# An encoder block on one core: an earlier fourth quarter, spread ends of the down-projection, a two-pass column block, and decay products shared between two engines

## The chip, the core and the metric

The kernel runs on one core of one Trainium2 chip. The core has a matrix engine (TensorE, PE in the profile), a vector engine (VectorE, DVE), a scalar engine (ScalarE, ACT), GpSimd (POOL), and queues that start DMA transfers (here SyncE, SP). Each engine works through its own list of instructions in order and waits at semaphores for the others. The metric is the device time of one execution in microseconds, the median over repeated runs.

## The reference

The block has three residual parts and a last normalisation, for 2048 positions and a width of 1024, all in float32:

```python
def block(x):
    x = x + mixer(x)            # short conv group + 4 gated-linear-attention heads, then w_out
    x = x + memory_cross_attention(x, mem)
    x = x + sq_relu_mlp(x)      # relu(rms_norm(x) @ w_up) ** 2 @ w_down
    return rms_norm(x, final_norm)

def gla_chunked(q, k, v, log_a):               # chunks of 64 positions, each head
    b = jnp.cumsum(la, axis=3)                 # running sum of the log decays in a chunk
    q_t = q * jnp.exp(b)                       # the two decay products that the change touches
    k_t = k * jnp.exp(-b)
    ...

def sq_relu_mlp(x, mlp_norm, w_up, w_down):
    h = rms_norm(x, mlp_norm) @ w_up           # 1024 -> 4096
    return jnp.square(jax.nn.relu(h)) @ w_down # 4096 -> 1024
```

The mixer's linear-attention part has four heads, forwards and backwards; the MLP has 4096 hidden units.

## The kernel before, in words

Activations are kept transposed, 128 channels on the partitions and positions along the free axis. Every float32 operand of a matrix product is cut in two by `split` (L117 and L118): ScalarE rounds it to a high part, VectorE subtracts that from it to get a low part, and `mm3` or `product` adds three matmuls, high by high, high by low and low by high. So behind every matmul there are a cast on ScalarE and a subtraction on VectorE, and those must come in time.

**Decays.** For each of the four heads a generator makes running sums of the log decays (`sums`: L397, the scans L400, copies L405 and L406, L407) and then, in `apply` (L422), multiplies their exponentials with k and q that come back from DRAM, 128x512 at a time, four products for each half of the positions, eight for a head. Its order is `sums(0)`, `apply(0)`, `sums(1)`, `apply(1)`. This runs beside the projections of the second half of the positions, whose results VectorE copies out of PSUM at L249. The matmuls of `mm3` stand at L145 to L147.

**MLP, up.** `token_side(hf)` and `weight_side(f)` make a scheme of seven products for a 2x2 block product (operands are sums and differences of quarters; for 16 values of f and two token halves hf). Four quarters of the tokens, a11, a12, a21, a22, are read from `x2d` and scaled (`quarter`, L956 and L960). Each quarter is kept in two 128x1024 tiles, either of the ST ring (two tiles of 8 KB a partition, `S2`) or of the RAW and CV rings (three each, `R2`). The weights of each f come into RAW and CV as well (L990). In a ring a tile is given out again when its last reader is done. a12 is needed by the second product in the list (`yield 2`); before, its load waits for the ST tile of a11.

**MLP, down.** The same scheme over four groups of hidden rows (`GROUPS`), 56 steps of four output tiles each (L1243); `half_steps` yields a step's operands, kept two steps ahead (`ahead`). Operand sums are made by GpSimd and VectorE (`combine`, through `add` at L928). The accumulators `acc` start as the residual, sixteen 128x1024 transfers from `x2d` (`load_acc`, L1218). `sums` holds partial sums u that belong to three of the four quarter outputs, so 24 additions `add(o, o, u)` follow the loop.

**Columns.** Four hidden tiles (`REST`) fit in no group. They are done behind the loop with plain `mm3`, in five column blocks of up to 512 positions: `column` adds 12 matmuls for each of eight output tiles d to `acc`, squares it, and sums the squares; `finish` makes the norm's factors and writes the block out. `between` runs the finish of the last block in between.

Where `tc.manual_schedule` is open (the five column blocks), PE and DVE keep the order in which the code is written; elsewhere, and for all other engines, a scheduler sets each engine's order from the program's dependencies and its own costs, so what a line issues can stand elsewhere on an engine than the code suggests.

Of the kernel before, what the change touches and what calls it, by code (L numbers as in the profile page):

```python
# [13 lines left out]
ALU = mybir.AluOpType  # L14
# [16 lines left out]
def block_kernel(ctx, tc, x, mem, wm, wv, wlg, wlog, wout, wxk, wxv, wxqT, wxo, wup, wdn,  # L31
# [342 lines left out]
    def gla_decay(h, res):  # L374
# [35 lines left out]
        def apply(hf):  # L410
# [4 lines left out]
            for T, z in ((K[hf], zk), (Q[hf], zq)):  # L415
                for bi in range(2):
# [5 lines left out]
                    nc.vector.tensor_tensor(out=T[:, sl], in0=T[:, sl], in1=r, op=ALU.mult)  # L422
# [541 lines left out]
    def token_side(hf):  # L964
# [5 lines left out]
        a21 = quarter(hf, 1, 0, S2())  # L970
        yield None
# [8 lines left out]
        a12 = quarter(hf, 0, 1, S2())  # L980
# [238 lines left out]

    halves = [slice(0, TB), slice(TB, 2 * TB)]  # L1220
# [3 lines left out]
    load_acc(range(4))  # L1224
    sums = [A4(F32, (P, 2, TB)) for _ in range(4)]
    for i in range(14 * len(GROUPS)):
# [3 lines left out]
        if i == 0:  # L1230
            load_acc(range(4, KT))
# [5 lines left out]
        for d in range(4):  # L1237
# [7 lines left out]
            o11, o21 = (acc[d][c][:, h] for h in halves)  # L1245
            o12, o22 = (acc[d + 4][c][:, h] for h in halves)
# [4 lines left out]
            for o in {1: (u,), 2: (o11,), 6: (u,), 5: (o22,), 3: (o12,), 7: (o21, o22), 4: (o21,)}[p]:  # L1251
                if p == 4:
                    add(o, o, ps, SUB)
                else:
                    add(o, ps, o)


    def rest_u(b):
        got = []
        for i in range(0, 4, 2):  # L1260
            t = (RAW() if i == 0 else CV()[:, :D]).rearrange("p (j t) -> p j t", j=2)
            for j in range(2):
                f = REST[i + j]
                nc.sync.dma_start(t[:, j], zu[f * P:(f + 1) * P, b * TB:(b + 1) * TB])
            hi, lo = (A4(F32R, (P, 2, TB)) for _ in range(2))
            split(t, hi, lo)
            got += [(hi[:, j], lo[:, j]) for j in range(2)]
        return got

    ur = [rest_u(0)]  # L1270
    wr = [load_w(wdn[f], T=G4) for f in REST]
    for d in range(4):
        for c in range(2):
            u = sums[d][:, c]
            for o in (acc[d][c][:, halves[1]], acc[d + 4][c][:, halves[0]], acc[d + 4][c][:, halves[1]]):
                add(o, o, u, eng=nc.vector)
# [13 lines left out]
    def column(us, c, cs, squares, between):  # L1290
# [3 lines left out]
        o = cs.start % TB  # L1294
        for d in range(KT):
            ds = slice(d * P, (d + 1) * P)
            ps = (PG if d % 2 == 0 else PS)()[:, :n]
            for j in range(4):
                mm3(ps, (wr[j][0][:, ds], wr[j][1][:, ds]), (us[j][0][:, o:o + n], us[j][1][:, o:o + n]), j == 0, j == 3)
# [94 lines left out]
```

## Time and profile before

| what | value |
|---|---|
| median of three runs | 2694.26 us (2693.18 to 2695.48) |
| profiled execution, its own time | 2702.45 us |
| its span | 2700.7 us |
| granted TensorE clock, mean | 0.983 |
| PE busy | 2592.5 us (96%) |
| VectorE busy | 1626.4 us (60%) |
| ScalarE busy | 933.2 us (35%) |
| GpSimd busy | 259.6 us (10%), 178 instructions |
| DMA | 353.26 MB, 131 GB/s in the mean |

Times in the profile are microseconds from the start of the span. A group's row gives the line, the engine, the operation, output<-inputs by the names of the tiles, partitions x elements, and the count, then busy time and mean nanoseconds of one. A timeline row begins with the start and the duration, and may end with the idle time ahead of it and what ended that, in brackets. A row of waits names who waited for whom, then the total in microseconds, the number of waits and the longest. PEclk is the clock that TensorE was granted, as a share of full speed. The stages lie at about 490 to 566 us (second half of the projections, with decays of heads 0 and 1), 1440 to 2038 (MLP up; its second token half from about 1727 on), 2034 to 2584 (MLP down), and 2584 to the end (column blocks).

### The profile page before, as it was taken

The page shows a single profiled execution, that of the slowest core. Times are in us where ns is not written, and L with a number is a line of the kernel's source. Part 1 is how long each engine was busy: PE and PEld are TensorE (multiplying, and loading weights), DVE is VectorE, ACT ScalarE, POOL GpSimd, SP SyncE. Part 2 cuts the span into 40 slices and gives each one's busy share as a digit, 9 for nine tenths or more (in the row PEclk, how much of TensorE's full clock was granted, in tenths as well). Part 3 has the DMA queues.
Part 4 walks back from the last instruction along what each step waited for, and adds up shares of the span by engine and source line. Part 5 has one row for each costly group of instructions (what it writes and reads, how often), then busy time and mean ns, then how long its engine had stood idle before and what let it go on. Part 6 is the DMA issues. An engine that isn't in the chain of part 4 may idle for free.

```text
span 2700.7 us, 34654 instructions
## 1 busy us (share of the span) xinstructions
PE 2592.5 (96%) x13560; PEld 2207.7 (82%) x13560; DVE 1626.4 (60%) x2502; ACT 933.2 (35%) x1432; POOL 259.6 (10%) x178
## 2 busy tenths in 40 slices
PE   7999999989989999999999999899999899999998
PEld 7898888877777787989997888788887788888877
DVE  6512363467766455344467657766556768687975
ACT  5411153434435343232234333433333223222232
POOL 0000000000010000000000000000003224243223
PEclk9999999999999999999999999999999999999999
DMA  7512354224435452111134333343338664555233
GB/s 253 179 61 69 101 185 162 81 88 121 135 104 175 145 183 94 52 43 48 48 115 166 106 113 106 110 159 107 112 121 290 220 197 150 179 168 174 95 106 110
DMA packets 198309, 353.26 MB, mean 131 GB/s; under 512 B 17345, under 2 KB 73793, under 8 KB 198145
## 3 DMA queue, kind: packets, MB, share of 16 engines
q1 hardware_dynamic: 198144, 351.05, 39.9%
q8 instruction: 106, 1.74, 0.3%
q14 instruction: 59, 0.48, 0.1%
HBM read 262.90 MB, written 88.08 MB: 130 GB/s over the span
## 4 chain that ended last, share of the span: by engine, by line
PE 77%; DVE 10%; DMA 6%; ACT 3%; issue 2%; POOL 0%; SPq 0%; DVEq 0%; POOLq 0%; ACTq 0%
PE ps L1013 12%; PE ps L145 9%; PE ps L147 9%; PE ps L146 9%; PE pg L1243 9%; PE ps L1243 9%; PE pg L1013 9%; PE pg L145 3%; PE pg L147 3%; PE pg L146 2%; DVE a L118 2%; DMA gt<-zv 2%; DVE g L118 1%; DVE st L474 1%; DVE g L400 1%
## 5 line engine op out<-in xcount | busy, mean ns | idle before, releaser
L145 PE MATMUL ps<-a,a 128*128 128x512 f32 (+1 forms) x840 | 306.0, 364 | 6.5 <-DVE t L249 5.9
L146 PE MATMUL ps<-a,a 128*128 128x512 f32 (+1 forms) x840 | 306.0, 364 | 0.0
L147 PE MATMUL ps<-a,a 128*128 128x512 f32 (+1 forms) x840 | 305.1, 363 | 0.0
L1243 PE MATMUL pg<-a,g 128*128 128x512 f32 x1176 | 288.6, 392 | 10.1 <-DVE a L928 7.2
L1013 PE MATMUL ps<-a,g 128*128 128x512 f32 x1152 | 284.5, 392 | 7.4 <-ACT a L117 4.4
L1243 PE MATMUL ps<-a,g 128*128 128x512 f32 x1176 | 284.8, 389 | 0.0
L1013 PE MATMUL pg<-a,g 128*128 128x512 f32 x1152 | 279.6, 390 | 1.7 <-ACT g L117 1.1
L1243 PEld LDWEIGHTS pg<-a,g 128*128 128x128 f32 x1176 | 221.7, 189 | 59.1 <-issue 7.6
L1013 PEld LDWEIGHTS ps<-a,g 128*128 128x128 f32 x1152 | 217.4, 189 | 54.1 <-ACT a L117 5.0
L1243 PEld LDWEIGHTS ps<-a,g 128*128 128x128 f32 x1176 | 220.8, 188 | 45.9
L1013 PEld LDWEIGHTS pg<-a,g 128*128 128x128 f32 x1152 | 216.4, 188 | 48.4 <-ACT g L117 2.0
L117 ACT CAST a<-raw 128x1024 fp32r<-128x1024 f32 (+1 forms) x126 | 127.9, 1022 | 346.0 <-PE ps L1243 112.1
L118 DVE TENSOR_TENSOR a<-raw,a 128x1024 fp32r<-128x1024 f32 (+1 forms) x126 | 156.0, 1246 | 117.3 <-ACT a L117 115.9
L117 ACT CAST g<-gt 128x512 fp32r<-128x512 f32 x180 | 103.8, 618 | 349.0 <-PE pg L1013 197.2
L145 PEld LDWEIGHTS ps<-a,a 128*128 128x128 f32 x840 | 161.6, 192 | 32.6 <-DVE t L249 4.7
L146 PEld LDWEIGHTS ps<-a,a 128*128 128x128 f32 x840 | 162.0, 193 | 23.2 <-issue 0.2
L147 PEld LDWEIGHTS ps<-a,a 128*128 128x128 f32 x840 | 161.7, 192 | 23.3 <-issue 0.2
L118 DVE TENSOR_TENSOR g<-gt,g 128x512 fp32r<-128x512 f32 x180 | 133.4, 780 | 44.7 <-ACT g L117 44.7
L928 POOL TENSOR_TENSOR gt<-gt,t 128x512 f32<-128x512 f32 x42 | 79.4, 1908 | 815.9 <-DMA t<-in_wdn 746.9
L928 DVE TENSOR_TENSOR t<-pg,t 128x512 f32<-128x512 f32 x64 | 44.2, 691 | 172.0 <-issue 126.3
L928 DVE TENSOR_TENSOR a<-pg,a 128x512 f32<-128x512 f32 (+1 forms) x128 | 84.1, 668 | 62.3 <-PE pg L1243 46.1
L118 DVE TENSOR_TENSOR g<-raw,g 128x1024 fp32r<-128x1024 f32 (+3 forms) x90 | 98.7, 1107 | 35.6 <-ACT g L117 35.5
(323 smaller groups left out, 5157.7 us busy)
## 6 DMA issues: line engine op xcount, KB each, us to landing
raw<-zu SPq DMA_DIRECT2D x64, 512.0 KB, 4.1
t<-in_wdn SPq DMA_DIRECT2D x84, 256.0 KB, 4.1
raw<-in_wm SPq DMA_DIRECT2D x32, 512.0 KB, 4.1
raw<-in_wup SPq DMA_DIRECT2D x32, 512.0 KB, 4.1
cv<-in_wup SPq DMA_DIRECT2D x32, 512.0 KB, 4.9
zu<-gt SPq DMA_DIRECT2D x64, 256.0 KB, 2.4
zu<-t SPq DMA_DIRECT2D x64, 256.0 KB, 3.9
cv<-zu SPq DMA_DIRECT2D x32, 512.0 KB, 5.0
```

What stands on the lines that cost most here:

```text
L117: mark["act"] = nc.scalar.copy(hi, src)
L118: nc.vector.tensor_tensor(out=lo, in0=src, in1=hi.bitcast(F32), op=ALU.subtract)
L145: nc.tensor.matmul(ps, lh, rh, start=first, stop=False)
L146: nc.tensor.matmul(ps, lh, rl, start=False, stop=False)
L147: mark["pe"] = nc.tensor.matmul(ps, ll, rh, start=False, stop=last)
L400: nc.vector.tensor_tensor_scan(out=Q[hf][:, sl], data0=reset, data1=K[hf][:, sl], initial=0.0, op0=ALU.mult, op1=ALU.add)
L474: nc.vector.scalar_tensor_tensor(out=St[r, a], in0=St[r, b], scalar=de[r, a:a + 1], in1=St[r, a], op0=ALU.mult, op1=ALU.add)
L928: eng.tensor_tensor(out=out, in0=a, in1=b, op=op)
L1013: nc.tensor.matmul(ps, W[w][:, ks], X[x][kt], start=first and kt + w + x == 0, stop=kt == 3 and w == 1, skip_group_check=not first)
L1243: nc.tensor.matmul(ps, l, r, start=not chained and k == 0 and l is wh and r is x[k][0], stop=k == n - 1 and l is wl, skip_group_check=chained)
```

## The change

Four things change.

First, a product of `apply` goes to GpSimd for heads 0 and 1 and stays on VectorE for heads 2 and 3: 16 of the 32 instructions move. Nothing else in the generator differs.

Second, in `token_side(1)` the quarter a12 is loaded right behind a21, into RAW and CV tiles; for the first half the code is as it was. On SyncE's queue, around the end of the first token half, this moves transfers. Before (raw and cv are the RAW and CV rings, st the ST ring, zu the hidden activations that go out, L990 the weights and L956 the quarters):

```order
L1019 DMA zu<-gt 128x512 x2
L1023 DMA zu<-t_13838 128x512
L990 DMA raw<-in_wup 128x1024
L1023 DMA zu<-t_13876 128x512
L990 DMA cv<-in_wup 128x1024
...
L1023 DMA zu<-t_14298 128x512
L990 DMA raw<-in_wup 128x1024
L990 DMA cv<-in_wup 128x1024
L956 DMA st<-x2d 128x2x512 x2
L1152 DMA st<-zu 128x2x512
```

And in the changed kernel, where L993 are the weights, from the same place on:

```order
L1022 DMA zu<-gt 128x512 x2
L1026 DMA zu<-t_13838 128x512
L956 DMA raw<-x2d 128x2x512
L1026 DMA zu<-t_13876 128x512
L956 DMA cv<-x2d 128x2x512
...
L1026 DMA zu<-t_13990 128x512
L993 DMA raw<-in_wup 128x1024
L1026 DMA zu<-t_14028 128x512
L993 DMA cv<-in_wup 128x1024
```

The two transfers of a12 stood, as st loads, behind four pairs of weight loads counted from the first of these rows; now they are a raw and a cv load in the place of the first of those pairs, and each pair of weights follows one place later.

Third, the beginning of the down-projection. The sixteen accumulator loads are issued at steps 0 and 2, eight each; before, eight were issued ahead of the loop and eight at step 0. Before, on SyncE's queue (a is an accumulator, t and gt tiles of the down weights, zu a hidden tile that is read back):

```order
L1171 DMA t_16721<-in_wdn 128x512
L1218 DMA a_16759<-x2d 128x1024
...
L1218 DMA a_16773<-x2d 128x1024
L1125 DMA cv<-zu 128x2x512
L1171 DMA gt<-in_wdn 128x512 x4
L1171 DMA t_16903<-in_wdn 128x512
```

In the changed kernel, from the first hidden tiles that the sums need:

```order
L1128 DMA raw<-zu 128x2x512
L1128 DMA cv<-zu 128x2x512
L1221 DMA a_16744<-x2d 128x1024
...
L1174 DMA t_16706<-in_wdn 128x512
L1221 DMA a_16750<-x2d 128x1024
...
L1221 DMA a_16758<-x2d 128x1024
L1174 DMA gt<-in_wdn 128x512 x4
```

The raw and cv tiles of the first hidden-row sum stand ahead of every accumulator, and the second eight accumulators, which stood ahead of the first gt weights, now come behind them and behind seven more weight transfers.

Fourth, the end of the down-projection. Operands of the first column block (`rest_u(0)`) and the first REST weights are asked for two steps before the loop ends. The 24 additions of u are made inside the first three column blocks, one for each d. The first column block goes through its eight output tiles twice: first with two of the four REST tiles, in all eight PSUM banks, then with the other two. The dictionary `goes` and `out_` say the same as the lines that they replace. On VectorE, before (g is a low part of a REST weight, the a rows with two a inputs are the additions of u, those with pg or ps take a product out of PSUM):

```order
L118 TENSOR_TENSOR g_20862<-raw,g_20861 128x1024
L928 TENSOR_TENSOR a_16709<-ps,a_16709 128x512
L928 TENSOR_TENSOR a_16773<-ps,a_16773 128x512
L118 TENSOR_TENSOR g_20868<-raw,g_20867 128x1024
L928 TENSOR_TENSOR a_16697<-a_16697,a_16711 128x512
L928 TENSOR_TENSOR a_16761<-a_16761,a_16711 128x512
...
L928 TENSOR_TENSOR a_16773<-a_16773,a_16714 128x512
L118 TENSOR_TENSOR a_20901<-raw,a_20900 128x1024
L118 TENSOR_TENSOR a_20908<-cv,a_20907 128x1024
L928 TENSOR_TENSOR a_16695<-pg,a_16695 128x512
```

In the changed kernel:

```order
L118 TENSOR_TENSOR g_20863<-raw,g_20862 128x1024
L928 TENSOR_TENSOR a_16758<-ps,a_16758 128x512
L928 TENSOR_TENSOR a_16943<-ps,a_16943 128x512
L118 TENSOR_TENSOR g_20869<-raw,g_20868 128x1024
L118 TENSOR_TENSOR a_20878<-raw,a_20877 128x1024
L118 TENSOR_TENSOR a_20885<-cv,a_20884 128x1024
L928 TENSOR_TENSOR a_16746<-a_16746,a_16696 128x512
L928 TENSOR_TENSOR a_16744<-pg,a_16744 128x512
L928 TENSOR_TENSOR a_16750<-a_16750,a_16697 128x512
L928 TENSOR_TENSOR a_16748<-ps,a_16748 128x512
L928 TENSOR_TENSOR a_16754<-a_16754,a_16698 128x512
L928 TENSOR_TENSOR a_16752<-pg,a_16752 128x512
```

The row of fourteen additions between the second weight and the first product is gone from there; each of them stands ahead of one product of the column block, and the splits of two weights and of the next operands come directly behind one another.

The diff, with the body of `rest_u` left out (it is moved up unchanged):

```diff
@@ -419,7 +419,7 @@
                     for o in (0, 64):
                         nc.sync.dma_start(r[o:o + 64], z[pr][r0:r0 + 64, c0:c0 + TB])
                     sl = slice(bi * TB, (bi + 1) * TB)
-                    nc.vector.tensor_tensor(out=T[:, sl], in0=T[:, sl], in1=r, op=ALU.mult)
+                    (nc.gpsimd if h < 2 else nc.vector).tensor_tensor(out=T[:, sl], in0=T[:, sl], in1=r, op=ALU.mult)
 
         sums(0)
         yield
@@ -968,6 +968,8 @@
         a11 = quarter(hf, 0, 0, S2())
         a22 = quarter(hf, 1, 1, R2())
         a21 = quarter(hf, 1, 0, S2())
+        if hf == 1:
+            a12 = quarter(hf, 0, 1, R2())
         yield None
         yield 1, operand(a11)
         yield 4, operand(a22)
@@ -977,7 +979,8 @@
         both(s, s, a11, ALU.subtract)
         yield 6, operand(s)
         both(a21, a11, a21, ALU.subtract)
-        a12 = quarter(hf, 0, 1, S2())
+        if hf == 0:
+            a12 = quarter(hf, 0, 1, S2())
         yield 2, operand(a12)
         yield 7, operand(a21)
         both(a12, a12, s, ALU.subtract)
@@ -1217,18 +1220,32 @@
                 acc[d][c] = A4()
                 nc.sync.dma_start(acc[d][c], x2d[d * P:(d + 1) * P, c * 1024:(c + 1) * 1024])
 
+    def rest_u(b):
...
     halves = [slice(0, TB), slice(TB, 2 * TB)]
     steps = half_steps()
     ahead = [next(steps)]
     acc = [[None, None] for _ in range(KT)]
-    load_acc(range(4))
     sums = [A4(F32, (P, 2, TB)) for _ in range(4)]
     for i in range(14 * len(GROUPS)):
         while len(ahead) < 3:
             ahead.append(next(steps, None))
         first, p, c, w, x = ahead.pop(0)
-        if i == 0:
-            load_acc(range(4, KT))
+        if i in (0, 2):
+            load_acc(range(2 * i, 2 * i + 4))
+        if i == 14 * len(GROUPS) - 2:
+            ur = [rest_u(0)]
+            wr = [load_w(wdn[REST[0]], T=G4)]
         n = len(x)
 
         chained = p in (2, 3)
@@ -1242,38 +1259,20 @@
                 for l, r in ((wh, x[k][0]), (wh, x[k][1]), (wl, x[k][0])):
                     nc.tensor.matmul(ps, l, r, start=not chained and k == 0 and l is wh and r is x[k][0],
                                      stop=k == n - 1 and l is wl, skip_group_check=chained)
-            o11, o21 = (acc[d][c][:, h] for h in halves)
-            o12, o22 = (acc[d + 4][c][:, h] for h in halves)
+            out_ = lambda dd, h: acc[dd][c][:, halves[h]]
             u = sums[d][:, c]
             if p == 1 and first:
                 nc.scalar.copy(u, ps)
                 continue
-            for o in {1: (u,), 2: (o11,), 6: (u,), 5: (o22,), 3: (o12,), 7: (o21, o22), 4: (o21,)}[p]:
+            goes = {2: ((d, 0),), 5: ((d + 4, 1),), 3: ((d + 4, 0),), 7: ((d, 1), (d + 4, 1)), 4: ((d, 1),)}
+            for o in [u] if p in (1, 6) else [out_(*g) for g in goes[p]]:
                 if p == 4:
                     add(o, o, ps, SUB)
                 else:
                     add(o, ps, o)
 
 
...
-    ur = [rest_u(0)]
-    wr = [load_w(wdn[f], T=G4) for f in REST]
-    for d in range(4):
-        for c in range(2):
-            u = sums[d][:, c]
-            for o in (acc[d][c][:, halves[1]], acc[d + 4][c][:, halves[0]], acc[d + 4][c][:, halves[1]]):
-                add(o, o, u, eng=nc.vector)
+    wr += [load_w(wdn[f], T=G4) for f in REST[1:]]
 
     def final_sums(sq, n, PT):
         m = n // P
@@ -1287,17 +1286,35 @@
         nc.vector.scalar_tensor_tensor(out=a, in0=a, scalar=g_fin[:, d:d + 1], in1=r, op0=ALU.mult, op1=ALU.mult)
         nc.sync.dma_start(out[d * P:(d + 1) * P, c * 1024 + cs.start:c * 1024 + cs.stop], a)
 
-    def column(us, c, cs, squares, between):
+    def column(us, c, cs, squares, between, passes=1):
 
         qs = []
         n = cs.stop - cs.start
         o = cs.start % TB
+        pss = []
+
+        def part(d, js):
+            ds = slice(d * P, (d + 1) * P)
+            for j in js:
+                mm3(pss[d], (wr[j][0][:, ds], wr[j][1][:, ds]), (us[j][0][:, o:o + n], us[j][1][:, o:o + n]), j == 0, j == 3)
+
+        for d in range(KT if passes == 2 else 0):
+            pss.append((PG if d % 2 == 0 else PS)()[:, :n])
+            part(d, (0, 1))
         for d in range(KT):
-            ds = slice(d * P, (d + 1) * P)
-            ps = (PG if d % 2 == 0 else PS)()[:, :n]
-            for j in range(4):
-                mm3(ps, (wr[j][0][:, ds], wr[j][1][:, ds]), (us[j][0][:, o:o + n], us[j][1][:, o:o + n]), j == 0, j == 3)
+            if passes == 1:
+                pss.append((PG if d % 2 == 0 else PS)()[:, :n])
+            part(d, (2, 3) if passes == 2 else range(4))
+            ps = pss[d]
             a = acc[d][c][:, cs]
+
+            if (c, cs.start) != (1, TB) and n == TB:
+                if cs.start == TB or d >= 4:
+                    add(a, a, sums[d % 4][:, c])
+                elif d < 4:
+                    dd = d + 4 * c
+                    late = acc[dd][1][:, halves[1]]
+                    add(late, late, sums[d][:, 1])
             add(a, ps, a)
             qs.append(GT()[:, :n])
             nc.scalar.activation(qs[-1], a, AF.Square)
@@ -1325,7 +1342,8 @@
         for n, (c, cs) in enumerate(blocks):
             if n + 1 < 4:
                 ur.append(rest_u(n + 1))
-            sq = column(ur[min(n, 3)], c, cs, nc.vector if n == len(blocks) - 1 else nc.gpsimd, todo)
+            sq = column(ur[min(n, 3)], c, cs, nc.vector if n == len(blocks) - 1 else nc.gpsimd, todo,
+                        2 if n == 0 else 1)
             for _ in todo or ():
                 pass
             todo = finish(c, cs, sq)
```

More of the change, by code (lines that the diff above doesn't have):

```diff
@@ L1218, in load_acc @@
                 nc.sync.dma_start(acc[d][c], x2d[d * P:(d + 1) * P, c * 1024:(c + 1) * 1024])
+    def rest_u(b):
+        got = []
+        for i in range(0, 4, 2):
+            t = (RAW() if i == 0 else CV()[:, :D]).rearrange("p (j t) -> p j t", j=2)
+            for j in range(2):
+                f = REST[i + j]
+                nc.sync.dma_start(t[:, j], zu[f * P:(f + 1) * P, b * TB:(b + 1) * TB])
+            hi, lo = (A4(F32R, (P, 2, TB)) for _ in range(2))
+            split(t, hi, lo)
+            got += [(hi[:, j], lo[:, j]) for j in range(2)]
+        return got
     halves = [slice(0, TB), slice(TB, 2 * TB)]
@@ L1255, in block_kernel @@
                     add(o, ps, o)
[L1258 to L1268, printed above, removed]
-    ur = [rest_u(0)]
-    wr = [load_w(wdn[f], T=G4) for f in REST]
-    for d in range(4):
-        for c in range(2):
-            u = sums[d][:, c]
-            for o in (acc[d][c][:, halves[1]], acc[d + 4][c][:, halves[0]], acc[d + 4][c][:, halves[1]]):
-                add(o, o, u, eng=nc.vector)
+    wr += [load_w(wdn[f], T=G4) for f in REST[1:]]
     def final_sums(sq, n, PT):
```

## The prediction

> **What bounds the kernel now.** I read the page's head first.
>
> ```profile
> span 2700.7 us, 34654 instructions
> PE 2592.5 (96%) x13560; PEld 2207.7 (82%) x13560; DVE 1626.4 (60%) x2502; ACT 933.2 (35%) x1432; POOL 259.6 (10%) x178
> raw<-in_wup SPq DMA_DIRECT2D x32, 512.0 KB, 4.1
> ```
>
> TensorE is busy for 96%, so the time is the time of its matmuls plus its idle stretches. An edit on another engine can win only what TensorE idles, or loses to a lower clock, at the place of the edit. So the second view is a table of stretches. Its columns are the stretch, its length, the busy time and count of PE, PEld, DVE, ACT and POOL, the granted clock, the DMA share and GB/s.
>
> ```profile
> core 0: us, PE busy (x) PEld busy (x) DVE busy (x) ACT busy (x) POOL busy (x), PEclk, DMA share, GB/s
> 514.00:532.00 18.00, 18.00 (x162) 18.00 (x161) 13.20 (x22) 12.12 (x12) 0.00 (x0) 1.00 0.43 145
> 532.00:562.00 30.00, 23.54 (x182) 22.96 (x181) 23.92 (x52) 14.71 (x15) 0.00 (x0) 0.94 0.33 102
> 1738.00:1758.00 20.00, 14.71 (x52) 11.35 (x51) 13.35 (x16) 9.94 (x13) 0.00 (x0) 0.83 0.44 127
> 1800.00:1820.00 20.00, 20.00 (x89) 16.49 (x89) 11.29 (x18) 7.31 (x12) 0.00 (x0) 1.00 0.41 131
> 2050.00:2060.00 10.00, 10.00 (x46) 8.29 (x45) 2.32 (x4) 5.48 (x10) 0.00 (x0) 1.00 1.03 410
> 2094.00:2114.00 20.00, 12.81 (x49) 10.13 (x48) 19.14 (x23) 4.50 (x5) 0.00 (x0) 0.83 0.83 280
> 2584.00:2604.00 20.00, 15.41 (x51) 10.85 (x51) 20.00 (x29) 4.09 (x5) 0.00 (x0) 0.83 0.43 108
> ```
>
> Count matmuls, not busy time, since a slow matmul counts as busy. The undisturbed stretch at 1800 has 89 of 128x512 in 20 us, 0.2247 us each. The three stretches like it at the places of the change have 52, 49 and 51, so they lose 37, 40 and 38 matmuls: **8.3, 9.0 and 8.5 us**. In each the clock is 0.83, so part of each loss is the slow clock after a long stop, which goes with the stop. The decays' stretch has 182 matmuls where the rate of the row before it (162 of 128x256 in 18 us, 0.111 us each) gives 270: **9.8 us**. All four together, 35.6 us, are a ceiling for what these edits can win at these places. What ends the longest waits in the MLP's two halves, from the list of waits (who for whom, total us, number, longest):
>
> ```profile
> PE ps L1013 <- ACT a L117: 4.4, 1, 4.4
> PE pg L1243 <- DVE a L928: 7.2, 1, 7.2
> ```
>
> **Part A, the quarter a12.** Its timeline, three engines together:
>
> ```profile
> 1724.28 0.33 SPq L990 DMA_DIRECT2D raw<-in_wup  x1
> 1728.59 1.22 DVE L118 TENSOR_TENSOR g<-raw,g 128x1024 fp32r<-128x1024 f32 x1
> 1733.87 1.22 DVE L928 TENSOR_TENSOR st<-st 128x1024 f32<-128x1024 f32 x1
> 1735.12 0.89 SPq L956 DMA_DIRECT2D st<-x2d  x2
> 1737.44 2.88 PE L1013 MATMUL pg<-a,g 128*128 128x512 f32 x12
> 1742.18 2.74 DVE L960 SCALAR_TENSOR_TENSOR st<-st,vec,rows 128x512 f32<-128x512 f32 x4 [5.29 <-DMA st<-x2d]
> 1744.73 0.51 PE L1013 MATMUL ps<-a,g 128*128 128x512 f32 x1 [4.41 <-ACT a L117]
> ```
>
> The load goes out at 1735.12, as the last reader of a11's tile ends (1733.87 + 1.22); it lands, is scaled until 1744.92 and cast, and TensorE, which was free at 1740.32, starts at 1744.73, at half clock for a while. In the changed kernel a12's transfers stand where the weights of the second half's f = 0 stood, two rounds of f earlier, so the load and the four scalings (2.74 us, on VectorE) are over some 40 us before. The price is one place for the weights: those of f = 1 now go out where 1724.28 stands, and land 4.1 us later (page row above) at 1728.4; with a cast (1.04 us, the ACT row under part C) their split can start at 1729.4 instead of 1728.59, so VectorE's list runs about 1 us late, to some 1738. Two splits of 1.22 us make a12's operands by 1740.4, against TensorE's 1740.32. No stop is left that is long enough to cost the clock. I keep 1 us for the a21 and a12 - s splits behind it, which VectorE now has to deliver without a pause: gain **7** of 8.3 (3 if the weights come late at each of the next f, 8.3 at most). GpSimd has no work in this stage (0.00 in both rows), so nothing there contends.
>
> **Part B, the start of the down-projection.**
>
> ```profile
> 2045.59 6.50 SPq L1218 DMA_DIRECT2D a<-x2d  x8
> 2059.10 4.31 SPq L1171 DMA_DIRECT2D t<-in_wdn  x4
> 2061.41 0.69 DVE L928 TENSOR_TENSOR a<-pg,a 128x512 f32<-128x512 f32 x1 [8.58 <-PE pg L1243]
> 2066.51 6.50 POOL L928 TENSOR_TENSOR gt<-gt,t 128x512 f32<-128x512 f32 x4 [646.65 <-DMA t<-in_wdn]
> 2074.02 7.42 DVE L118 TENSOR_TENSOR g<-gt,g 128x512 fp32r<-128x512 f32 x3
> 2081.37 4.58 DVE L118 TENSOR_TENSOR a<-st,a 128x1024 fp32r<-128x1024 f32 x2
> 2087.07 3.48 DVE L928 TENSOR_TENSOR st<-st,raw 128x1024 f32<-128x1024 f32 x1
> 2090.47 3.43 DVE L928 TENSOR_TENSOR st<-st,cv 128x1024 f32<-128x1024 f32 x1
> 2102.80 4.95 PE L1243 MATMUL pg<-a,g 128*128 128x512 f32 x12 [7.19 <-DVE a L928]
> ```
>
> The stop of 7.19 us names an addition out of PSUM on VectorE, which is itself at the end of a queue. While GpSimd works (from 2066.51 on), VectorE's instructions with two inputs in SBUF are stretched: three weight splits take 7.42 us, and without GpSimd six of them took 3.8:
>
> ```profile
> L118 DVE TENSOR_TENSOR g<-gt,g 128x512 fp32r<-128x512 f32 x6 | 3.8, 684 | 0.0
> ```
>
> So these three lose 7.42 - 2.05 = 5.4 us, the two st splits 4.58 - 2.44 = 2.1 and the two st sums 6.91 - 2.44 = 4.5 (1.22 alone, in part A): 12.0 us in a row. Yet just before, VectorE had idled 8.58 us in one wait. GpSimd starts late because the down weights stand behind eight accumulators of 512 KB, while the transfers are full (DMA share 1.03, 410 GB/s). The change takes those eight, 4 MB or 10 us at 410 GB/s, from ahead of GpSimd's inputs. The same 12 us of stretching then falls mostly where VectorE idles. I take **8** of 9.0. The other end: GpSimd's first sums now come while the first weight splits run, around 2034, and those feed the first matmuls; two of them stretched to 2.47 (7.42/3) cost 3.6 us there, and if in turn nothing is won at 2102, this part loses 2. So -2 to 9.
>
> **Part C, the end.**
>
> ```profile
> 2591.16 1.04 ACT L117 CAST g<-raw 128x1024 fp32r<-128x1024 f32 x1
> 2592.33 1.22 DVE L118 TENSOR_TENSOR g<-raw,g 128x1024 fp32r<-128x1024 f32 x1
> 2593.46 8.51 DVE L928 TENSOR_TENSOR a<-a,a 128x512 f32<-128x512 f32 x14
> L928 POOL TENSOR_TENSOR gt<-gt 128x512 f32<-128x512 f32 x21 | 27.4, 1307 | 63.7 <-ACT gt L1303 63.4
> ```
>
> Two things hold TensorE in 2584 to 2604: the weight splits, the last of which ends at 2593.55, and 14 additions behind them that keep the first product out until 2601.97. The first pass over eight banks needs two weights alone and has 8 x 6 matmuls, 10.8 us at 0.2247, which reaches past the splits of the other two. What the change pays: ten of the 24 additions ran beside full matmuls before and now all 24 stand in the columns. In the second pass TensorE gives a product each 6 x 0.2247 = 1.35 us; VectorE needs 8.51/14 = 0.61 for the addition and about the same for the product, 1.2 us, which fits. But GpSimd sums the squares at 1.31 us each (last row), and as part B shows the two-input addition and GpSimd's instruction hold each other up, so 0.61 + 1.31 = 1.9 us for each d against 1.35. Over eight d, GpSimd's sum ends 8 x 0.57 = 4.6 us late; the next block has 12 matmuls, 2.7 us, for each d, so it catches up there, and TensorE meets the delay only where it needs the squares. I charge 2.5 us: gain **6** of 8.5 (2 if all 4.6 and as much again land on TensorE's path, 8.5 if none).
>
> **Part D, the decay products.**
>
> ```profile
> L422 DVE TENSOR_TENSOR g<-g,gt 128x512 f32<-128x512 f32 x16 | 10.0, 687 | 3.2 <-ACT g L411 3.2
> L400 DVE TENSOR_TENSOR_SCAN g<-cst,g 128x256 f32<-128x256 f32 x16 | 9.7, 672 | 0.1
> 527.40 2.50 DVE L422 TENSOR_TENSOR g<-g,gt 128x512 f32<-128x512 f32 x4 [0.88 <-ACT g L411]
> 529.81 1.22 DVE L397 TENSOR_TENSOR g<-g,g 128x1024 f32<-128x1024 f32 x1
> 534.36 0.42 DVE L249 COPY t<-ps 128x256 f32<-128x256 f32 x1
> 557.72 0.58 PE L145 MATMUL ps<-a,a 128*128 128x256 f32 x1 [4.53 <-DVE t L249]
> ```
>
> The 16 products leave VectorE, 10.0 us in all, 2.5 for each half of a head; on GpSimd they take 1.31 each. TensorE waits here for the copies at L249, which stand behind `sums` in VectorE's list, which stood behind the products. Alone, L397 and what follows would start at once, and the copy at 534.36 would come 2.5 + 0.88 us sooner. But now four products on GpSimd (5.2 us) run at the same time as L397, four scans and L407, which all have two inputs in SBUF. If each pair excludes one another as in part B, the chain of 4.6 us (529.81 to 534.36) becomes 4.6 + 5.2 = 9.8 from 526.5 on, and ends at 536.3, 1.9 later than now; twice, -3 or -4. If scans run freely, it ends 3 us earlier and the 4.53 us wait with its slow clock is mostly gone: +8. No row shows a scan beside GpSimd, but VectorE's 128x512 subtractions and 128x1024 sums above all stretched, so I take the value near the lock with some slack, **0**.
>
> The Trainium skill, in "SBUF — State Buffer", section "Who interferes with whom", says that a VectorE instruction with two SBUF inputs contends with a GpSimd instruction that reads SBUF, and that the later one waits for the whole of the earlier. The rows of part B agree for subtractions and sums; for a scan no run here shows it. By that rule D would be the 0 or the loss, and the sum 21; by a rule that excepted scans, 29.
>
> **Sum.** 7 + 8 + 6 + 0 = 21 us. The profiled execution took 2702.45 us (1.75 more than its span) and would take 2681.5; it stands 8.2 above the median of the runs, and I carry the difference: 2694.26 - 21 = **2673**.
>
> **Rivals.** *More comes free:* scans don't contend, and the column block adds no waits. For it: only subtractions and sums were seen to stretch. Against it: a scan reads two SBUF tiles like them. It adds 8 (D) and up to 4 (B and C whole): 2694.3 - 33 = 2661, 2657 to 2666.
> *The start of the down-projection gives nothing:* GpSimd's early sums stretch the first weight splits, at 2034, by as much as they spare at 2102; with half of A gone too, the gain is 3.5 + 0 + 6 = 9.5 and less where the column waits are at their bound: 2681 to 2689. For it: VectorE stands behind ScalarE's casts there anyway, and the DMA is full.
> *It doesn't do what it says:* a12 comes early, but the weights behind it late, so TensorE stops for w instead, and the other stops pass to the next item in VectorE's queue. Gain under 5: 2690 to 2694, within the 0.2% (5.4 us) that a measurement here can tell from no change.
> *Slower:* one mechanism, that VectorE and GpSimd exclude each other whole wherever the change put them side by side, in the decays and the columns. VectorE then loses 16 x 1.29 = 20.6 less the 10.0 it was spared, and 24 x 1.31 = 31 at the additions, 42 in all. It decides once more than 21 of these reach TensorE; all of it gives 2694 + 42 - 21 = 2715. Against it: VectorE idles 40% of the time, and in the later column blocks a d takes 2.7 us.
>
> **Chances.** The forecast 0.50 (its own range 2666 to 2682), more comes free 0.18, the start gives nothing 0.17, no effect 0.09, slower 0.06. The range of 2658 to 2690 holds the first three but for their edges; it leaves out the last two. Faster 0.85, same 0.09, slower 0.06.
>
> **What would show it.** A: 1738 to 1758 with 80 matmuls or more and clock 1.00, L960 of a12 before 1710. B: GpSimd's first sum before 2060, no PE wait over 2 us between 2090 and 2110. C: no clock under 1.00 in 2584 to 2604, additions of u one by one, and a wait of 1 to 4 us near the first `final_sums`. D: scans beside GpSimd of clearly over 672 ns; at 672 the first rival holds. Wrong is the forecast if PE's wait at any of A to C stays over 4 us, or if new stops of more than 5 us appear in the weights after a12 or in the second column block.

## The result

The changed kernel takes 2679.74 us in the median (2678.59 to 2681.76, 4 runs) against 2693.72 for the kernel before (2692.69 to 2695.48, 4 runs): ratio 0.9949, 95% interval 0.9933 to 0.9964. Timed again beside its variants it gave 0.9944 (0.9930 to 0.9957). So it is 14 to 15 us faster. The forecast was 21 us faster, 2673 in a range of 2658 to 2690: the direction and the range held, and the forecast gain was one and a half times the measured one.

Its page begins, in the same form as before:

```profile
span 2676.8 us, 34723 instructions
PE 2582.6 (96%) x13560; PEld 2202.0 (82%) x13560; DVE 1629.3 (61%) x2486; ACT 933.6 (35%) x1432; POOL 278.9 (10%) x194
```

Busy times hardly differ. GpSimd has 16 more instructions, VectorE fewer, and yet VectorE's busy time rose from 1626.4 to 1629.3 us. What differs is in the stretches (columns as before):

```profile
core 0: us, PE busy (x) PEld busy (x) DVE busy (x) ACT busy (x) POOL busy (x), PEclk, DMA share, GB/s
532.00:562.00 30.00, 23.29 (x173) 22.91 (x172) 22.51 (x40) 14.52 (x15) 14.77 (x12) 0.87 0.38 119
1738.00:1758.00 20.00, 20.00 (x90) 16.54 (x89) 19.37 (x26) 11.19 (x18) 0.00 (x0) 1.00 0.73 246
2024.00:2034.00 10.00, 8.11 (x26) 5.53 (x25) 5.25 (x8) 4.68 (x8) 1.70 (x1) 0.83 0.88 300
2070.00:2090.00 20.00, 20.00 (x90) 16.36 (x89) 19.89 (x19) 6.39 (x8) 9.39 (x4) 1.00 0.86 297
2094.00:2114.00 20.00, 20.00 (x90) 16.55 (x89) 14.28 (x17) 6.19 (x8) 8.98 (x7) 1.00 0.69 235
2584.00:2604.00 20.00, 18.43 (x88) 14.92 (x87) 17.18 (x23) 6.00 (x9) 11.88 (x9) 1.00 0.07 26
```

Three of the four stops are gone: 90, 90 and 88 matmuls at full clock where there were 52, 49 and 51. In the decays' stretch the change did the opposite: 173 matmuls instead of 182, and a mean clock of 0.87 instead of 0.94. And there is a new stop at about 2025: 26 matmuls in 10 us at a clock of 0.83, where the kernel before has 46 at full clock.

Both kernels have 13,560 matmuls, so the k-th matmul can be looked up in two traces and its start compared. The difference of the two starts changes only where one kernel loses or wins. This table gives that change in microseconds, stage by stage (stages by the clock of the first trace of before); each row is one profiled execution, set against the first profile of before. The rows below the first three are the experiments.

| profile | 10–512 | decays 512–586 | 586–1469 | A 1694–1841 | start of down 2000–2065 | B 2065–2195 | C 2570–2608 | columns after it, 2608–2693 |
|---|---|---|---|---|---|---|---|---|
| before, again | +0.2 | -0.2 | -2.8 | -0.5 | +0.9 | -0.8 | -0.4 | -0.1 |
| changed | +0.6 | +2.3 | -5.3 | -7.0 | +3.0 | -11.6 | -8.9 | +3.7 |
| changed, again | +0.7 | +2.2 | -1.5 | -6.9 | +0.1 | -11.3 | -7.9 | +5.2 |
| A alone | -0.9 | -0.4 | -4.9 | -7.8 | 0.0 | -0.6 | 0.0 | 0.0 |
| B alone | -1.3 | +1.1 | -7.5 | -0.4 | +0.4 | -11.3 | -1.7 | -0.5 |
| C alone | +0.5 | +2.2 | -5.3 | -0.4 | +1.0 | -0.9 | -8.9 | +5.2 |
| D alone | +0.7 | +2.1 | -6.0 | +0.1 | 0.0 | -0.2 | +0.3 | -0.5 |
| changed, D undone | -4.2 | 0.0 | -4.9 | -7.8 | +0.4 | -11.6 | -8.9 | +3.9 |
| D undone, no additions of u in the columns | -1.0 | +0.2 | -2.7 | -7.0 | +0.8 | -10.7 | -8.9 | -0.1 |
| only the second half's products on GpSimd | -1.3 | -2.4 | -7.8 | -7.0 | +0.8 | -10.4 | -8.9 | +5.2 |
| the same, 8 additions in the loop | -0.2 | -1.7 | -8.8 | -7.9 | +1.8 | -10.8 | -8.9 | +3.4 |
| the same, 16 additions in the loop | -1.3 | -4.3 | +1.4 | -7.0 | +0.6 | -10.9 | -8.9 | +2.0 |
| the last, GpSimd's share for all four heads | -1.9 | -1.2 | -3.5 | -7.8 | +1.3 | -10.7 | -8.9 | +0.6 |

The stages left out (1469–1694, 1841–2000, 2195–2570) never differ by more than 0.1. In 586–1469 (attention, projections, many short waits) even two profiles of one kernel differ by 2.8 and 3.8 us; nothing in the edits touches it. The first profile of before was long there, which is part of why it took 2702.45 us while the median run took 2694.

### The profile page after: what moved, and what is told of

Read it like the earlier page. It is cut to its first block, busy times and chain, and to the rows that moved or that the text cites. A ratio compares the mean times of both kernels' runs of the same rounds, so it can differ in the third digit from the quotient of the medians.

```text
span 2676.8 us, 34723 instructions
## 1 busy us (share of the span) xinstructions
PE 2582.6 (96%) x13560; PEld 2202.0 (82%) x13560; DVE 1629.3 (61%) x2486; ACT 933.6 (35%) x1432; POOL 278.9 (10%) x194
## 4 chain that ended last, share of the span: by engine, by line
PE 78%; DVE 10%; DMA 5%; ACT 3%; issue 3%; POOL 1%; SPq 0%; DVEq 0%; POOLq 0%; ACTq 0%
PE ps L1016 12%; PE pg L1260 10%; PE ps L1260 10%; PE ps L145 9%; PE ps L147 9%; PE ps L146 9%; PE pg L1016 9%; PE pg L145 3%; PE pg L147 3%; PE pg L146 3%; DVE a L118 2%; DMA gt<-zv 2%; DVE g L400 1%; DVE st L474 1%; DVE a L928 1%
## 5 line engine op out<-in xcount | busy, mean ns | idle before, releaser
L118 DVE TENSOR_TENSOR a<-raw,a 128x1024 fp32r<-128x1024 f32 (+1 forms) x128 | 161.8, 1270 | 125.3 <-ACT a L117 123.4
L153 POOL TENSOR_TENSOR sm<-sm,nhalf 128x2 f32<-128x2 f32 (+1 forms) x26 | 24.3, 933 | 991.0 <-DVE sm L151 991.0
L117 ACT CAST g<-raw 128x1024 fp32r<-128x1024 f32 (+3 forms) x90 | 85.4, 959 | 95.3 <-PE ps L146 17.4
```

Of the source, the lines that this page charges most:

```text
L117: mark["act"] = nc.scalar.copy(hi, src)
L118: nc.vector.tensor_tensor(out=lo, in0=src, in1=hi.bitcast(F32), op=ALU.subtract)
L153: nc.gpsimd.tensor_tensor(out=r, in0=v, in1=nhalf[:, :n], op=ALU.pow)
```

## The experiments

**The four parts, one at a time.** Each is the kernel before with one part.

A:

```diff
+        if hf == 1:
+            a12 = quarter(hf, 0, 1, R2())
...
-        a12 = quarter(hf, 0, 1, S2())
+        if hf == 0:
+            a12 = quarter(hf, 0, 1, S2())
```

> The kernel before with the earlier quarter a12 alone. Theory (the prediction's step A, and the two traces, whose distance shrinks by 7.0 us across this place): 7 us less than before, ratio 0.9974; 1738 to 1758 at clock 1.00 with some 89 matmuls; nothing changes at 2094 and 2584. Rival (the weights behind a12 come late instead): under 3 us, with new waits of TensorE for casts of weights between 1730 and 1800.

Measured 2687.68 against 2696.83 us, ratio 0.9965 (0.9953 to 0.9977); at its own place 7.8 us in the trace. The theory holds, the rival falls: no new wait for weights. (One wait of 0.53 us for the split of a12's operand is new.)

B:

```diff
-    load_acc(range(4))
...
-        if i == 0:
-            load_acc(range(4, KT))
+        if i in (0, 2):
+            load_acc(range(2 * i, 2 * i + 4))
```

> The kernel before with the accumulator loads at steps 0 and 2 alone (the changed lookup of the outputs comes with it, since an accumulator may not exist yet when it is named). Theory: the stop at 2095 to 2107 goes (about 9 us), and a new one of 2 to 3 us appears at the first down-projection matmul, because the first weights stand behind four hidden-tile loads: net 6 to 9, ratio 0.997 to 0.9978. Rival: without the earlier a12 the queue stands otherwise and the stop of 3 us at the start is not there: 9 us, 0.9967. Second rival (GpSimd's sums stretch VectorE's splits at another place): under 3 us.

Measured 2681.74 us, ratio 0.9953 (0.9941 to 0.9964). At its place it wins 11.3 us, more than the theory's 9, and the stop at the start does not appear, as the first rival said. But that rival's reason was wrong: SyncE's queue has the same order here as in the changed kernel. The profile of B alone at the two places:

```profile
2020.00:2034.00 14.00, 13.74 (x55) 9.64 (x55) 7.00 (x11) 5.66 (x10) 4.78 (x2) 1.00 0.97 328
2094.00:2114.00 20.00, 20.00 (x90) 16.53 (x90) 14.54 (x16) 6.19 (x8) 10.59 (x8) 1.00 0.69 233
```

Here the first three weights landed nearly in time (0.4 us lost); in the first profile of the changed kernel TensorE waited 1.9 us for them:

```profile
2016.58 0.36 SPq L1128 DMA_DIRECT2D cv<-zu  x1
2018.71 1.58 SPq L1174 DMA_DIRECT2D t<-in_wdn  x3
2026.54 0.62 ACT L117 CAST g<-t 128x512 fp32r<-128x512 f32 x1 [3.31 <-DMA t<-in_wdn]
2027.21 3.84 PE L1260 MATMUL pg<-a,g 128*128 128x512 f32 x9 [1.89 <-ACT g L117]
```

The weights stand behind four loads of hidden tiles and one accumulator. From the issue to the first cast 7.8 us pass, and TensorE waits, then runs at half speed for a moment (nine matmuls in 3.84 us). In the second profile of the changed kernel 5.8 us pass, and this stage cost 0.1 us; in the other runs with part B it cost 0.4 to 1.8, and two runs without part B show 0.9 and 1.0. So this stop of 3 us is a margin that one execution missed, not a fixed cost.

C:

```diff
+        if i == 14 * len(GROUPS) - 2:
+            ur = [rest_u(0)]
+            wr = [load_w(wdn[REST[0]], T=G4)]
...
+        for d in range(KT if passes == 2 else 0):
+            pss.append((PG if d % 2 == 0 else PS)()[:, :n])
+            part(d, (0, 1))
...
+                    add(a, a, sums[d % 4][:, c])
...
+                    add(late, late, sums[d][:, 1])
```

> The kernel before with the two-pass column block, the spread additions and the earlier first operands alone. Theory: 8.5 to 8.9 us won at 2584 to 2604, 4 lost in waits for the sums of squares in the next blocks: 4.6 us net, ratio 0.9983. Rival (the prediction's price of the new waits, 2.5): 6 us, 0.9978. Second rival (all of GpSimd's delay lands on the path): 0 to 2.

Measured 2692.24 us, ratio 0.9985 (0.9977 to 0.9994), 4 us. In the trace 8.9 us are won at the end of the loop and 5.2 given back in the columns. The theory holds.

D:

```diff
-                    nc.vector.tensor_tensor(out=T[:, sl], in0=T[:, sl], in1=r, op=ALU.mult)
+                    (nc.gpsimd if h < 2 else nc.vector).tensor_tensor(out=T[:, sl], in0=T[:, sl], in1=r, op=ALU.mult)
```

> The kernel before with the decay products of heads 0 and 1 on GpSimd alone. Theory (scans and GpSimd's products exclude each other in turn): a scan beside GpSimd takes 672 + about 950 ns, the half-rate stretch at 557 stays, 2 to 3 us slower than before, ratio 1.0010. Rival (scans run freely): 672 ns throughout, 3 to 8 us faster, 0.997 to 0.999.

Measured 2698.79 against 2696.83 us, ratio 1.0012 (1.0004 to 1.0021): slower by 2 to 3 us, and 2.1 us at its place. The rival of free scans falls.

**The changed kernel again, and without D.**

> The changed kernel once more, timed beside its variants. The four parts alone gave ratios 0.9965, 0.9953, 0.9985 and 1.0012; if they add, 0.9915 (23 us). Rival (part B wins less when a12 is early, since the first down weights then come 3 us late, and the pieces in the traces sum to 17.7): 0.9935. The first measurement said 0.9949.

Measured 2680.12 us, 0.9944 (0.9930 to 0.9957). The interval shuts out the product of the parts, 0.9915, and holds the rival's 0.9935. The rival's reason does not hold, though: in this profile the start of the down-projection cost 0.1 us. At their places in the traces the parts alone sum to 20.3 us (7.8 + 10.9 + 3.7 - 2.1), and this profile shows 18.6, so most of why the timed parts do not add stays open.

> The changed kernel with all decay products on VectorE again. Theory: 3 us faster than the changed kernel (its part alone cost 0.0012 of the time), one half-rate stretch instead of two between 532 and 566. Rival (D's cost was noise): no difference.

Undoing D (the diff above, reversed):

Measured 2674.13 us (2668.82 to 2675.35), ratio to before 0.9918 (0.9905 to 0.9932), so 6 us faster than the changed kernel beside it. The two intervals barely touch, so the rival falls; with some 3.5 us of uncertainty on each, the theory's 3 is not shut out. The table places 2.2 us in the decays. Whatever is more is not placed: the stages 10–512 and 586–1469 were shorter in this profile, but they vary by about as much between two profiles of one kernel.

**Why D costs: the lock or GpSimd's speed?**

```diff
-                    (nc.gpsimd if h < 2 else nc.vector).tensor_tensor(...)
+                    (nc.gpsimd if h < 2 and hf == 1 else nc.vector).tensor_tensor(...)
```

> The changed kernel with GpSimd making only the products of the second half (no scan follows these) of heads 0 and 1, eight instead of sixteen. Theory (what costs is the lock between scans and products): scans at 0.6 us again, no cost against all on VectorE, so 2 to 4 us faster than the changed kernel. Rival (GpSimd's slower products cost by themselves, their results come late): some 1 to 2 us of cost stay, TensorE waits for what the products feed.

Measured 2671.23 us, 0.9912 (0.9898 to 0.9926): 9 us faster than the changed kernel, and as fast as with all products on VectorE (the intervals overlap). At its place in the traces the difference to the changed kernel is 4.6 us. The scans' group on VectorE between 514 and 570, first in the changed kernel, then here, and GpSimd's products in the same order:

```profile
L400 DVE TENSOR_TENSOR_SCAN g<-cst,g 128x256 f32<-128x256 f32 x16 | 17.9, 1179 | 0.1
L422 POOL TENSOR_TENSOR g<-g,gt 128x512 f32<-128x512 f32 x16 | 22.4, 1434 | 142.2 <-ACT g L411 142.2
```

```profile
L400 DVE TENSOR_TENSOR_SCAN g<-cst,g 128x256 f32<-128x256 f32 x16 | 9.7, 673 | 0.1
L422 POOL TENSOR_TENSOR g<-g,gt 128x512 f32<-128x512 f32 x8 | 10.1, 1293 | 150.8 <-ACT g L411 150.8
```

With no scan beside them, both engines are at their own speed (673 and 1293 ns); GpSimd's products are nearly twice as slow as VectorE's (687 ns) and yet cost TensorE nothing. In the changed kernel, too, the trace shows nobody waiting for a product of GpSimd between 500 and 640; up to 570 TensorE waits there for the copies at L249, which stand behind the stretched scans, and for nothing else. So it is the lock, the scans and GpSimd's products holding each other up, and not GpSimd's speed, that costs. The stretch 532 to 562 now has 199 matmuls, more than the 182 of before:

```profile
532.00:562.00 30.00, 25.53 (x199) 25.30 (x199) 20.36 (x46) 16.02 (x17) 10.09 (x8) 0.94 0.35 111
```

**What the columns pay for.** As the changed kernel without D, and the additions left out of the columns, so that three of the four quarter outputs lack u:

```diff
-            if (c, cs.start) != (1, TB) and n == TB:
-                if cs.start == TB or d >= 4:
-                    add(a, a, sums[d % 4][:, c])
-                elif d < 4:
-                    ...
-                    add(late, late, sums[d][:, 1])
```

> As the kernel with all decay products on VectorE, and the 24 additions of u left out of the columns (part of the computation is left out: three of the four quarter outputs lack u). It measures what the additions cost there. Theory (two-input additions and GpSimd's sums of squares hold each other up): the three waits of the column blocks, 4.2 us in all, go, and additions stay single on VectorE; 3 to 5 us faster than with them. Rival (the second pass's 1.35 us for a d is too short for squares at 1.3 us on GpSimd in any case): 0 to 2 us.

Measured 2667.31 us, ratio to before 0.9901 (0.9888 to 0.9915), against 0.9918 with the additions. The two intervals overlap, so the traces decide: the 3.9 us that the columns gave back with the additions are gone (-0.1). The theory holds, and the short second pass alone costs nothing.

Then two kernels that compute everything, with GpSimd's products as in the last experiment but one, and eight or sixteen of the additions moved into the loop's last group (the second is shown):

```diff
+            if i >= 14 * (len(GROUPS) - 1) and p in (6, 4):
+                to = {(6, 0): (d + 4, 0, 0), (6, 1): (d, 1, 1), (4, 0): (d, 0, 1), (4, 1): (d + 4, 0, 1)}[(p, c)]
+                o = acc[to[0]][to[1]][:, halves[to[2]]]
+                add(o, o, sums[d][:, to[1]])
...
-            if (c, cs.start) != (1, TB) and n == TB:
+            if (c, cs.start) == (1, 0):
```

> GpSimd makes only the second half's products of heads 0 and 1, and the eight additions of u that stood in the first column block stand in the loop, behind the third product of the last group. Theory (two-input additions in the short second pass delay the sums of squares): the wait at the end of the first block, 3.2 us against the kernel before, goes; the later ones of 1 to 2.5 us stay; 3 us faster than without that move (2671), about 2668. Rival (the additions only move their delay into the loop's last steps, where VectorE is busy for 21 of 24 us): no gain, a new wait of TensorE between 2530 and 2570.

Measured 2669.23 against 2696.98 us, ratio 0.9892 (0.9875 to 0.9908). The columns give back 3.4 instead of 5.2 us: the loss at the end of the first block fell from 2.1 to 0.4 us and did not go. The second block's additions follow at once; with those moved too, in the next run, it is gone.

> The same with sixteen of the 24 additions in the loop, four behind each of four steps of the last group; only the third block keeps its eight. Theory: 4 to 5 us faster than 2671, about 2666 to 2667, as when the additions are left out, if the loop has the 10 us of VectorE to spare. Rival: TensorE waits in the loop, 2668 or more.

Measured 2669.19 us, 0.9894 (0.9879 to 0.9909). The columns give back 2.0, and the loop before them is as long as ever (the stage to 2570 differs by 0.0): VectorE had the time to spare. The time lies where the rival had it and not at the theory's 2666 to 2667, but the rival's reason, waits in the loop, is not in the trace. The 1.4 us that the columns won over the last run do not show in the timed medians, whose intervals are some 4 us to either side.

> The last one with GpSimd making the second half's products of all four heads. Theory: heads 2 and 3 gain as heads 0 and 1 did where a product stood ahead of copies that TensorE waits for, 0 to 3 us more; rival: their products are needed soon after, so GpSimd's 1.3 us each is late, 1 to 3 us slower.

With GpSimd's share extended to heads 2 and 3 (`if hf == 1`): 2670.92 us, 0.9899 (0.9884 to 0.9914). Neither the gain nor the loss can be told from no difference.

**Was the first profile of before long by chance?**

> The kernel before, profiled once more. Theory (the first profile of it was long by chance in stages that no edit touches): 586 to 1469 takes some 5 us less than in the first profile, as in most profiles of the variants, and the places of the four edits take the same time within 1 us. Rival (the difference of 5 us there comes from the edits): 586 to 1469 as in the first profile within 1 us.

Its profiled execution took 2698.78 us, and 586–1469 was 2.8 us shorter than in the first profile: between theory and rival. The four places agree within 0.9 us, so the readings at the places stand, and the stages that no edit touches vary by some microseconds from execution to execution.

The kernels with eight or sixteen additions in the loop beat both kernels: 0.9892 and 0.9894 of the time before, against 0.9944 to 0.9949 for the change as it was made.

## Why the prediction was right or wrong

**Part A, 7 us: right.** Nine profiles with it show 6.9 to 7.9. The places named are in the changed kernel's trace:

```profile
1674.71 1.40 DVE L960 SCALAR_TENSOR_TENSOR raw<-raw,vec,rows 128x512 f32<-128x512 f32 x2
1721.77 0.33 SPq L993 DMA_DIRECT2D raw<-in_wup  x1
1735.89 1.22 DVE L118 TENSOR_TENSOR a<-raw,a 128x1024 fp32r<-128x1024 f32 x1
1737.46 2.66 PE L1016 MATMUL ps<-a,g 128*128 128x512 f32 x11
```

a12 is scaled at 1674.7, 67 us earlier; the weights go out one place later; a12's first split ends at 1737.1, and TensorE goes on at 1737.46 without a wait. (All stands 2 us earlier than in the trace of before.) The step between 6.9 and 7.9 is a slow stretch near 1725, behind two waits of 0.64 and 1.18 us. Five of the nine profiles have it, and so do three of the five without part A, with waits as long; so it is not a cost of the part.

**Part B, 8 us: right in mechanism, too small at its place, 10.4 to 11.6.** What was mis-sized is the ceiling: the sum counted the stretch 2094 to 2114 alone, 9.0 us, where the first profile of the changed kernel wins 9.3. The same late VectorE had already held TensorE between 2070 and 2090 in the kernel before, which the prediction left out of the ceiling:

```profile
2070.00:2090.00 20.00, 18.71 (x79) 14.35 (x79) 20.00 (x11) 6.62 (x10) 20.00 (x10) 1.00 0.56 196
```

79 matmuls, ten less than the 89 of an undisturbed stretch, and the table's method puts the gain between 2065 and 2094 at 2.3 us. GpSimd's st sums, in the kernel before and then in the changed one, moved ahead of the splits:

```profile
2072.98 3.38 POOL L928 TENSOR_TENSOR st<-st,raw 128x1024 f32<-128x1024 f32 x1
```

```profile
2020.95 2.40 POOL L928 TENSOR_TENSOR st<-st,raw 128x1024 f32<-128x1024 f32 x1 [603.28 <-DMA raw<-zu]
```

So they stretched none of the weight splits that the lower bound was made from. The rest of the 12 us of stretching did not only move, as the prediction had it: in the second group VectorE's own st sums found GpSimd idle. In the kernel before they took 3.48 and 3.43 us, in the changed kernel:

```profile
2090.54 1.21 DVE L928 TENSOR_TENSOR st<-st,raw 128x1024 f32<-128x1024 f32 x1
2091.67 1.21 DVE L928 TENSOR_TENSOR st<-st,cv 128x1024 f32<-128x1024 f32 x1
```

The rival in which the start of the down-projection gives nothing fell. A loss at the start did come, 3.0 us in one profile, but by late weights, not by the stretching that the prediction had named; with it part B was 8.6, and 11.2 in the second profile.

**Part C, 6 us: mis-sized, 3.7 to 5.2 in most profiles and 2.7 in one.** The gain of 8.5 was right (7.9 to 8.9). The charge for new waits was 2.5, and they cost 3.7 to 5.2; without the additions they are gone. The prediction priced the first block's delay (4.6 us) and then assumed that the next blocks, with 2.7 us for each d, catch up. The first block's end cost 2.1 us, near the whole charge. What the sum put at nothing are the ends of the second and the third block: 1.0 us each in the first profile, and 2.5 for the third in five of the eight profiles that keep its additions, where a slow stretch follows the wait. Each of these blocks has eight additions of its own, and `finish` of the block before adds two-input work in between. The group of additions, spread over the columns of the changed kernel:

```profile
L928 DVE TENSOR_TENSOR a<-a,a 128x512 f32<-128x512 f32 x24 | 24.5, 1022 | 0.0
```

That is 1.02 us each in the mean, where the fourteen of the kernel before have 0.69 in the same view. The chain from the first block's squares runs:

```profile
2591.21 1.57 DVE L118 TENSOR_TENSOR a<-raw,a 128x1024 fp32r<-128x1024 f32 x1
2592.70 2.31 DVE L118 TENSOR_TENSOR a<-cv,a 128x1024 fp32r<-128x1024 f32 x1
2597.72 0.15 DVE L151 TENSOR_SCALAR sm<-ps 128x4 f32<-128x4 f32 x1
2597.95 1.39 POOL L153 TENSOR_TENSOR sm<-sm,nhalf 128x4 f32<-128x4 f32 x1 [4.03 <-DVE sm L151]
```

And TensorE's waits between 2580 and 2660:

```profile
PE ps L1281 <- POOL gt L928: 1.5, 2, 1.0
PE pg L169 <- POOL sm L153: 1.5, 1, 1.5
```

At the first block's end TensorE waits not for the squares but for the norm's factors (1.5 us): L151, a tiny instruction of 0.15 us, stands in VectorE's list behind two stretched splits and the second block's first additions, and TensorE's next step behind L151 and L153. At the ends of the second and third block it does wait for GpSimd's last sum of squares, as the prediction had it (0.5 and 1.0 us).

**Part D, 0 us: wrong, a loss of 2.2 us at its place and 2 to 6 in the time.** Its lock was described rightly and then softened ("the value near the lock with some slack"). The rows of the kernel before and of the changed kernel:

```profile
531.07 2.44 DVE L400 TENSOR_TENSOR_SCAN g<-cst,g 128x256 f32<-128x256 f32 x4
534.92 0.35 PE L145 MATMUL ps<-a,a 128*128 128x256 f32 x1 [1.41 <-DVE t L249]
```

```profile
527.98 6.24 POOL L422 TENSOR_TENSOR g<-g,gt 128x512 f32<-128x512 f32 x4 [126.93 <-ACT g L411]
528.21 6.56 DVE L400 TENSOR_TENSOR_SCAN g<-cst,g 128x256 f32<-128x256 f32 x4
536.18 0.36 PE L145 MATMUL ps<-a,a 128*128 128x256 f32 x1 [2.14 <-DVE t L249]
```

Four scans took 6.56 instead of 2.44 us. The prediction's full lock gave 1.9 us of delay for the copy behind; the wait grew by 0.7, from 1.41 to 2.14. What the prediction missed is the clock: the longer wait was followed by a half-rate stretch that the kernel before does not have there, and the one behind the next wait was longer. The stretches 538 to 544 and 562 to 568, before and changed:

```profile
538.00:544.00 6.00, 5.47 (x46) 5.46 (x46) 2.97 (x9) 4.04 (x5) 0.00 (x0) 1.00 0.71 216
562.00:568.00 6.00, 6.00 (x44) 5.62 (x43) 3.70 (x6) 3.12 (x5) 0.00 (x0) 1.00 0.61 183
```

```profile
538.00:544.00 6.00, 6.00 (x42) 6.00 (x42) 0.05 (x1) 5.97 (x8) 3.97 (x4) 0.77 0.64 192
562.00:568.00 6.00, 6.00 (x43) 6.00 (x42) 1.75 (x3) 1.10 (x2) 3.63 (x3) 0.78 0.16 52
```

Followed matmul by matmul, the loss comes in three steps: 0.7 us in the wait, 0.7 by 540 (0.77 of the clock over 6 us is 1.4 us of lost work, less a wait of 0.5 us at L432, and a little more idle time, that the changed kernel does not have), and 0.8 between 560 and 562. The second profile of the changed kernel and D alone show the same three steps (0.7, 0.7, 0.9 and 0.7, 0.7, 0.6). Two cautions. The last step is not D's alone: B alone, without D, loses 1.4 us there, with a wait as long as before. And C alone, which has no part of D either, also shows +2.2 in 512–586; but it loses nothing up to 568, and all of it behind a wait of 2.5 us for a DMA at 574, where the profiles with D lose nothing. So the first two steps are seen in all three profiles in which GpSimd works beside the scans, and in none of the eleven others.

The rule that the prediction weighed, from the Trainium skill, "SBUF — State Buffer", section "Who interferes with whom" (a VectorE instruction with two SBUF inputs and a GpSimd one that reads SBUF exclude each other), is now shown for scans too: 2.44 us of scans and 5.0 of products (four with no scan beside them), 7.4 in turn, took 6.8 us together, so they ran in turn but for some 0.6 us.

**The sum.** 21 became 18.5 at the places (7.0 + 8.6 + 5.2 - 2.3 in the first profile; 18.6 in the second), 17.5 against the second profile of before, and 14 to 15 in the median. That the sum at the places came near 21 is in part luck: B won 0.6 to 3.2 us more than its term, and that made up for some of what C (0.8 to 3.3) and D (2.3) fell short. The terms were taken from one profile and set against another execution's median, 8 us shorter. Some of the 3 to 5 us between the places and the median may be D's unplaced cost; the rest stays open.

The other rivals: that more comes free fell with the scans; that the change doesn't do what it says fell with A and B; the slower one had the right mechanism, the lock, at the right two places, and a price far too high: 2.2 and 3.7 to 5.2 us of it reached TensorE, not 42.

## What to carry to other kernels

Work could be moved from VectorE to GpSimd for nothing here where VectorE beside it was idle or had an operand in PSUM, and it cost more than it spared where VectorE was doing two-input SBUF work: the eight products behind the scans were free on GpSimd, and the eight beside the scans cost TensorE time. Before moving, list what stands next to the moved work on the other engine. When a delay is priced, follow it through every block that repeats the same work, and not only through the first. And when a wait is priced, see whether it brings one more stretch of slow clock: here that cost as much again as the wait.

## What the runs showed of the hardware that was not expected

A scan, one of whose inputs is a constant tile, is stretched by GpSimd as a plain subtraction is: 672 to 1179 ns in the mean over sixteen, of which half had a neighbour (8 x 1.64 and 8 x 0.61 us).

The length of a wait did not decide alone whether a slow stretch followed. At 536 the wait of 2.1 us was followed by one in all three profiles with part D as it was made, and the wait of 1.4 us in none of the eleven others. But near 1725 waits of 0.6 and 1.2 us were followed by one in eight of fourteen profiles, and near 555 a wait of 3.0 us was followed by full clock up to 568 in the three runs with eight or sixteen additions in the loop, and by 0.79 between 556 and 562 in the run with the second half's products on GpSimd and no additions in the loop. What else decides stays open.

Three transfers of 256 KB, 7.8 us from the first issue to the first cast, stopped TensorE in one execution of the changed kernel; in the next, by the same queue order, it was 5.8 us.
